# Experts of a mixture-of-experts block: the gated values split on one engine, and four weight splits moved

## The chip, the core and the metric

The kernel runs on one core of one Trainium2 chip. The core has five engines that work side by side, each with its own queue of instructions in program order: TensorE (PE in the rows: matrix products; PEld is its weight load), VectorE (DVE), ScalarE (ACT), GpSimd (POOL) and SyncE (SP, which here only issues transfers). The metric is the device time of one execution in microseconds (us), lower is better, the median of several runs.

## What is computed

One transformer block over 2048 tokens of width 1024, in float32. Token mixers (retention and dilated attention) come first; they take the first three quarters of the time and the change does not touch them. Then every token is routed to 2 of 16 experts, and each expert does

```python
def expert_block(args):
    xblk, e = args
    hid = jax.nn.silu(xblk @ w_gate[e]) * (xblk @ w_up[e])
    return hid @ w_down[e]
```

with `w_gate` and `w_up` 1024 x 512 and `w_down` 512 x 1024 for each expert. The weighted results are added up by token, and a layer norm ends the block.

## The kernel before

**Three products for one.** A float32 product is done as three fast ones. An operand `a` is split into a rounded part `hi` (type fp32r) and a remainder `lo = a - hi`; the product is `hi*hi + hi*lo + lo*hi` (`passes`). `split` (lines 86 to 89) makes the two parts: ACT copies into `hi`, which rounds, and DVE subtracts (lines 88 and 89, which are the lines of every split in the trace, whatever is split).

**One expert after the other.** `MoE.run` goes through 16 experts, each with up to 256 tokens in the main path. For expert e, `blocks` runs four products `gate_up(m)`, m = 0 to 3: 48 matmuls each (line 1286) that give 128 of the 512 gate columns and 128 of the 512 up columns, transposed, side by side in one PSUM bank. After `gate_up(m)` the code writes `hidden(m - 1)` (line 1290): ACT takes silu of the gate half into a tile `s` (L1292), DVE multiplies by the up half (L1293), and `split` puts the parts of the result into `self.h`. Then `part` (line 1313) multiplies by the down weights: first k = 0, 1, 2 for four banks in turn, later k = 3. The very first nine matmuls need `h` of k = 0, 1 and 2 in that order, three matmuls each.

**Two ways to the end of an expert.** If the expert has at most 256 tokens, `two` (line 1550) turns the next expert's gathered tokens (`turn`: 16 transposes at L1261, four banks, each split by ACT and DVE) and then does k = 3. If it has more, `three` (line 1526) does another block of 128 tokens as well. In this run experts 1, 2, 4, 5, 6, 9, 12, 13 and 14 go through `two`, and 3, 7, 8, 10 and 11 through `three`; experts 0 and 15 have code of their own. After either, `rows` scales the four finished banks: ACT does it (L1329) and GpSimd adds the rows to the output in HBM (a scatter that reads and writes, L1229); for e = 3, 7, 11, 15 DVE does it (L1321). The next expert's `gate_up(0)` uses the bank that `rows` reads first.

**Weights.** `weights(n)` (line 1208) splits the next n pieces of the weight queue. A piece is 0.5 MB in one of four raw buffers; ACT and DVE split it, and then SP may ask for the piece that is four further on, into the same buffer (`issue`, L1205 for gate and up, L1206 for down). In the order of the queue, and with names that are used below, an expert's twelve pieces are: D0 to D3, its own down weights (split at m = 0 and m = 1); A0, A1, B0, B1, C0, C1, E0, E1, the next expert's gate and up weights for m = 0, 1, 2, 3. Four further on means: the split of A frees the buffer for C, B for E, C for D0 and D1 of the next expert, E for D2 and D3, D for the next A and B.

**Norms between.** After the experts 3, 7 and 11 a generator `fin` does the last layer norm of finished rows, a step at a time: one after each of m = 0, 1, 2 and one at the end of the expert, through the next three experts. A step is one to three passes of DVE over 1024 columns (L859, L867, L1415, L1417), with small work and a scatter on GpSimd. At m = 2 GpSimd also gathers the next expert's tokens (`fetch`, L1224), after the step's scatter.

In this part every engine works strictly in the order in which the code is written (`manual_schedule`), so an instruction that waits holds up all behind it on its engine.

Of the kernel before, what the change touches and what calls it, by code (L numbers as in the profile page):

```python
# [40 lines left out]
class Ring:  # L41
# [4 lines left out]
    def next(self):  # L46
        v = self.views[self.i % len(self.views)]
        self.i += 1
        return v
# [36 lines left out]
def split(nc, hi, lo, src, sub=None):  # L86

    nc.scalar.activation(hi, src, AF.Copy)  # L88
    (sub or nc.vector).tensor_sub(lo, src, hi)  # L89
# [799 lines left out]
def layer_norm(g, x, st, gain, shift, two):  # L889

    v = g.nc.vector.tensor_add
    for _ in layer_norm_steps(g, x, st, gain, shift, EPS, (g.nc.gpsimd.tensor_add if two else v, v)):
        pass
# [274 lines left out]
class MoE:  # L1168
# [120 lines left out]

    def hidden(self, m, ps):  # L1290
        nc, s = self.g.nc, self.sr.next()
        nc.scalar.activation(s, ps[:, :256], AF.Silu)  # L1292
        nc.vector.tensor_mul(s, s, ps[:, 256:])  # L1293
        split(nc, *(t[:, m, :] for t in self.h), s)

    def down(self, h, idx, tag="main", sums=None, then=None, wait=True):

# [8 lines left out]
    def banks(self, blocks, tag="main"):  # L1306
        return [(b, j, self.g.bank(tag)) for b in blocks for j in range(2)]
# [167 lines left out]
    def blocks(self, e, wg, idx, fin):  # L1475

        p = []
        for m in range(4):
            p.append(self.gate_up(wg[m]))
            if m == 3 and e < NE - 1:  # L1480
                self.hint(e)
            if m:
                self.hidden(m - 1, p[m - 1])
            self.weights((2, 2, 1, 1)[m])
            if m < 3:
                next(fin, None)
            if m == 2:
                self.fetch(e + 1)
                for b in range(2) if e % 4 == 3 else ():
                    self.gather(self.sums[b], self.g.d_z, idx[:, b, 0:1])  # L1490
                if e % 4 == 3 and e < NE - 1:
                    self.list(e // 4)
        return p[3]
# [55 lines left out]

    def two(self, e, ps):  # L1550

        self.weights(4)
        self.turn(e + 1)
        self.part(self.h, ps, (3,))

    def next_block(self, e):
        self.gather(self.xm, self.g.d_x1, self.ir[(e + 1) % 8][:, 2, 0:1])
# [201 lines left out]
```

## Time and profile before

| | |
|---|---|
| median of 3 runs | 3071.51 us (3070.02 to 3075.76) |
| the profiled execution: its time | 3069.23 us |
| its span, first to last instruction | 3067.5 us |
| granted TensorE clock, mean over the span | 0.978 of full |
| the 16 experts | from about 2308 us to the end |

The profile counts busy time by engine, and a busy TensorE hides its waits only if one asks for them. So it is read in three steps: the waits of PE in the experts, the instructions around each of them in order of time, and the transfers that those instructions wait for. Times in rows are microseconds from the start of the span, first the start, then the duration; the bracket is the idle time of the engine just before, and what ended it.

### The profile page before, as it was taken

The page shows a single profiled execution, that of the slowest core. Times are in us where ns is not written, and L with a number is a line of the kernel's source. Part 1 is how long each engine was busy: PE and PEld are TensorE (multiplying, and loading weights), DVE is VectorE, ACT ScalarE, POOL GpSimd, SP SyncE. Part 2 cuts the span into 40 slices and gives each one's busy share as a digit, 9 for nine tenths or more (in the row PEclk, how much of TensorE's full clock was granted, in tenths as well). Part 3 has the DMA queues.
Part 4 walks back from the last instruction along what each step waited for, and adds up shares of the span by engine and source line. Part 5 has one row for each costly group of instructions (what it writes and reads, how often), then busy time and mean ns, then how long its engine had stood idle before and what let it go on. Part 6 is the DMA issues. An engine that isn't in the chain of part 4 may idle for free. (4 is left out here: it accounts for less than half of the span.)

```text
span 3067.5 us, 44091 instructions
## 1 busy us (share of the span) xinstructions
PE 2924.9 (95%) x16140; PEld 2522.2 (82%) x16140; DVE 1427.3 (47%) x3257; ACT 975.4 (32%) x1945; POOL 665.7 (22%) x720
## 2 busy tenths in 40 slices
PE   8999999999999999999889999989998999989996
PEld 6887888888888888888668888878788988878885
DVE  3222433233335523334535666556555476444565
ACT  3221233223333322332123333333224444233342
POOL 0001311122113322100222212222433133122233
PEclk9999999999999999999899999999999999999998
DMA  6445956855776675545854444356737768365684
GB/s 208 147 176 158 201 144 156 182 140 139 157 167 165 174 163 145 143 117 173 287 202 134 155 155 139 127 178 206 145 124 214 253 211 282 112 191 166 208 264 157
DMA packets 449148, 534.16 MB, mean 174 GB/s; under 512 B 183153, under 2 KB 292849, under 8 KB 446818
## 3 DMA queue, kind: packets, MB, share of 16 engines
q1 hardware_dynamic: 261538, 417.78, 42.9%
q0 software_dynamic: 187328, 112.79, 16.1%
q8 instruction: 156, 2.56, 0.4%
q14 instruction: 126, 1.03, 0.1%
HBM read 378.12 MB, written 151.76 MB: 173 GB/s over the span
## 5 line engine op out<-in xcount | busy, mean ns | idle before, releaser
L144 PE MATMUL bank_main<-h,h 128*128 128x512 f32 x3936 | 1022.0, 404 | 9.1 <-ACT h L88 5.3
L144 PEld LDWEIGHTS bank_main<-h,h 128*128 128x128 f32 x3936 | 718.6, 191 | 147.9 <-ACT h L88 7.3
L361 ACT ACTIVATE at<-at,at 128x256 f32<-128x256 f32 (+2 forms) x384 | 174.4, 455 | 542.2 <-DVE at L359 514.6
L1286 PE MATMUL bank_main<-moe,m2w 128*128 128x256 f32 x2304 | 280.2, 283 | 7.5 <-DVE moe L1321 4.8
L1286 PEld LDWEIGHTS bank_main<-moe,m2w 128*128 128x128 f32 x2304 | 278.3, 192 | 10.2 <-issue 6.0
L359 DVE CUSTOM_DVE_ANT_0 at<-bank_att,at 128x256 f32<-128x256 f32 (+2 forms) x384 | 125.0, 363 | 210.7 <-PE bank_att L352 141.4
L1313 PE MATMUL bank_main<-mw,moe 128*128 128x512 f32 x744 | 190.7, 410 | 22.7 <-ACT moe L88 22.6
L1081 PE MATMUL bank_main<-m2w,m 128*128 128x512 f32 x768 | 195.2, 407 | 1.4 <-DVE m L89 1.4
L1313 PEld LDWEIGHTS bank_main<-mw,moe 128*128 128x128 f32 x744 | 141.2, 195 | 60.4 <-ACT moe L88 28.1
L744 PE MATMUL bank_main<-m1r,m1r 128*128 128x512 f32 x672 | 189.7, 415 | 0.0
L379 PEld LDWEIGHTS bank_att<-at,at 128*128 128x128 f32 (+1 forms) x1280 | 168.6, 191 | 15.7 <-DVE at L371 4.3
L1081 PEld LDWEIGHTS bank_main<-m2w,m 128*128 128x128 f32 x768 | 144.1, 193 | 34.3 <-DVE m L89 2.6
L89 DVE TENSOR_TENSOR h<-h,h 128x1024 fp32r<-128x1024 f32 x108 | 133.3, 1239 | 80.6 <-ACT h L88 80.0
L379 PE MATMUL bank_att<-at,at 128*128 128x64 f32 (+1 forms) x1280 | 164.1, 267 | 3.2 <-DVE at L371 3.1
L381 DVE COPY at<-bank_att 128x128 f32<-128x128 f32 x192 | 55.4, 289 | 218.0 <-PE bank_att L379 214.4
L352 PE MATMUL bank_att<-at,at 128*128 128x256 f32 (+2 forms) x768 | 152.9, 326 | 3.8 <-DVE at L381 3.8
L352 PEld LDWEIGHTS bank_att<-at,at 128*128 128x128 f32 x768 | 142.2, 234 | 14.3 <-DVE at L381 4.7
L320 POOL DMA_DIRECT2D at<-d_q x96 | 77.7, 812 | 347.5 <-PE bank_att L352 338.9
L744 PEld LDWEIGHTS bank_main<-m1r,m1r 128*128 128x128 f32 x672 | 125.2, 188 | 25.1
L319 POOL DMA_DIRECT2D at<-d_k x64 | 51.1, 815 | 418.9 <-PE bank_att L352 208.2
L89 DVE TENSOR_TENSOR m2w<-mw,m2w 128x1024 fp32r<-128x1024 f32 x78 | 96.0, 1237 | 94.8 <-ACT m2w L88 89.1
L88 ACT ACTIVATE h<-h 128x1024 fp32r<-128x1024 f32 x108 | 113.4, 1055 | 78.6 <-PE bank_main L144 44.9
(293 smaller groups left out, 4398.4 us busy)
## 6 DMA issues: line engine op xcount, KB each, us to landing
mw<-in_w_gu_dram SPq DMA_DIRECT2D x98, 512.0 KB
h<-in_w_in_dram SPq DMA_DIRECT2D x92, 512.0 KB
mw<-in_w_dn_dram SPq DMA_DIRECT2D x49, 512.0 KB
at<-d_q POOLq DMA_DIRECT2D x96, 256.0 KB
at<-d_k POOLq DMA_DIRECT2D x64, 256.0 KB
at<-d_va SPq DMA_DIRECT2D x240, 64.0 KB
moe<-in_w_gu_dram SPq DMA_DIRECT2D x30, 512.0 KB
d_o<-at SPq DMA_DIRECT2D x192, 66.0 KB
```

Source lines behind the costliest of these rows:

```text
L88: nc.scalar.activation(hi, src, AF.Copy)
L89: (sub or nc.vector).tensor_sub(lo, src, hi)
L144: self.g.nc.tensor.matmul(ps, s[:, k, c], m[:, k % 2, :], start=k + n == 0, stop=k * 3 + n == 23)
L320: done.append(nc.gpsimd.dma_start(Q[i][:, c], ap3(g.d_q, order * 1024 * T + o, [[512 * T, 2], [T, 64], [1, 512]])))
L352: nc.tensor.matmul(ps[:, e, :nk], queries(Q[e]), keys(k), start=n == 0, stop=n == 1)
L359: nc.vector.tensor_tensor_reduce(out=pe, in0=ps[:, e, :nk], in1=bv, scale=1.0, scalar=3e38, op0=OP.add, op1=OP.min, accum_out=ot[:, 128 + ...
L361: nc.scalar.activation(pe, pe, AF.Exp, scale=-1.0, bias=ot[:, 128 + e:129 + e], accum_out=ot[:, 130 + e:131 + e])
L379: nc.tensor.matmul(po[:, 64 * e:64 * e + 64], pt[:cw, e, c, :], v[:cw, c, 64 * e:64 * e + 64], start=c == 0, stop=c == nch - 1)
L744: nc.tensor.matmul(ps, a[:, kk:kk + 128], w[:, c], start=k == ks[0] and i == 0, stop=k == ks[-1] and i == 2)
L1081: nc.tensor.matmul(ps[j], a[:, kk], w[:, c], start=k + i == 0, stop=k * 3 + i == 23)
L1286: nc.tensor.matmul(ps[:, 256 * u:256 * u + 256], x[:, k, c], y[:, k, :], start=k + i == 0, stop=k * 3 + i == 23)
L1313: self.g.nc.tensor.matmul(p, a[:, k, 128 * b:128 * b + 128], w[:, 512 * j:512 * j + 512], start=k + i == 0, stop=k * 3 + i == 11)
```

## The change

`hidden` no longer uses `split`. ACT still does silu. DVE then multiplies twice, once into `hi` (the write rounds) and once in place, and subtracts. ACT's copy of 256 columns is gone, 60 times, and DVE has one more multiplication, 60 times.

Four splits stand elsewhere in each expert, in the same order of pieces: A0 moves from m = 2 to m = 3, in front of A1; in `two`, C0 and C1 move from ahead of `turn` to behind it and behind the last products. (`three` is not changed but for A0.)

```diff
     def hidden(self, m, ps):
         nc, s = self.g.nc, self.sr.next()
+        hi, lo = (t[:, m, :] for t in self.h)
         nc.scalar.activation(s, ps[:, :256], AF.Silu)
+        nc.vector.tensor_mul(hi, s, ps[:, 256:])
         nc.vector.tensor_mul(s, s, ps[:, 256:])
-        split(nc, *(t[:, m, :] for t in self.h), s)
+        nc.vector.tensor_sub(lo, s, hi)
...
-            self.weights((2, 2, 1, 1)[m])
+            self.weights((2, 2, 0, 2)[m])
...
     def two(self, e, ps):
 
-        self.weights(4)
+        self.weights(2)
         self.turn(e + 1)
         self.part(self.h, ps, (3,))
+        self.weights(2)
```

ACT at the end of expert 1, path `two` (B0, B1, C0, C1 are `m2w_14801` and `mw_14981`; the row with x4 is the splitting of the turned tokens; L1329, in the changed kernel L1331, is `rows`; `m2w_14795` is E). Before:

```order
L88 ACTIVATE m2w_14801<-mw_14993 128x1024
L88 ACTIVATE m2w_14801<-moe_17005 128x1024
L88 ACTIVATE mw_14981<-mw_14991 128x1024
L88 ACTIVATE mw_14981<-mw_14992 128x1024
L88 ACTIVATE moe_17022<-bank_att 128x4x128 x4
L1586 UNCONDITIONAL_BRANCH
L1329 ACTIVATE moe_17024<-bank_main,moe_17014 128x512 x4
L88 ACTIVATE m2w_14795<-mw_14993 128x1024
```

and now:

```order
L88 ACTIVATE m2w_14801<-mw_14993 128x1024
L88 ACTIVATE m2w_14801<-moe_17005 128x1024
L88 ACTIVATE moe_17022<-bank_att 128x4x128 x4
L88 ACTIVATE mw_14981<-mw_14991 128x1024
L88 ACTIVATE mw_14981<-mw_14992 128x1024
L1589 UNCONDITIONAL_BRANCH
L1331 ACTIVATE moe_17024<-bank_main,moe_17014 128x512 x4
L88 ACTIVATE m2w_14795<-mw_14993 128x1024
```

The two copies of C now stand between the turned tokens and `rows`.

DVE in expert 4, from the split of D3 (`moe_17005` into `mw_14990`) to the parts of `hidden(2)` (`moe_17010` is `lo` of `h`, `moe_17009` is `hi`; L867, L1415, L859 and L1417 are steps of a norm). Before:

```order
L89 TENSOR_TENSOR mw_14990<-moe_17005,mw_14989 128x1024
L867 BN_AGGR moe_17050<-moe_17050 128x2
L1415 SCALAR_TENSOR_TENSOR moe_17054<-moe_17054,moe_17050,moe_17044 128x1024
L859 BN_STATS moe_17048<-moe_17055 128x6 x2
L1293 TENSOR_TENSOR moe_17026<-moe_17026,bank_main 128x256
L89 TENSOR_TENSOR moe_17010<-moe_17026,moe_17009 128x256
L89 TENSOR_TENSOR m2w_14802<-mw_14991,m2w_14801 128x1024
L1417 SCALAR_TENSOR_TENSOR moe_17054<-moe_17054,moe_17050,moe_17045 128x1024
L867 BN_AGGR moe_17048<-moe_17048 128x2
L1415 SCALAR_TENSOR_TENSOR moe_17055<-moe_17055,moe_17048,moe_17044 128x1024
L1293 TENSOR_TENSOR moe_17025<-moe_17025,bank_main 128x256
L89 TENSOR_TENSOR moe_17010<-moe_17025,moe_17009 128x256
```

and now, from the first multiplication of `hidden(1)` on:

```order
L1294 TENSOR_TENSOR moe_17009<-moe_17026,bank_main 128x256
L1295 TENSOR_TENSOR moe_17026<-moe_17026,bank_main 128x256
L1296 TENSOR_TENSOR moe_17010<-moe_17026,moe_17009 128x256
L1419 SCALAR_TENSOR_TENSOR moe_17054<-moe_17054,moe_17050,moe_17045 128x1024
L867 BN_AGGR moe_17048<-moe_17048 128x2
L1417 SCALAR_TENSOR_TENSOR moe_17055<-moe_17055,moe_17048,moe_17044 128x1024
L1294 TENSOR_TENSOR moe_17009<-moe_17025,bank_main 128x256
L1295 TENSOR_TENSOR moe_17025<-moe_17025,bank_main 128x256
L1296 TENSOR_TENSOR moe_17010<-moe_17025,moe_17009 128x256
L89 TENSOR_TENSOR m2w_14802<-mw_14991,m2w_14801 128x1024
L89 TENSOR_TENSOR m2w_14802<-mw_14992,m2w_14801 128x1024
```

The subtraction for A0 (`m2w_14802` from `mw_14991`) has moved behind `hidden(2)`.

## Rows read from the trace of the kernel before

**Rows 1.** The page: busy time of each engine, its share of the span, and its instructions.

```profile
PE 2924.9 (95%) x16140; PEld 2522.2 (82%) x16140; DVE 1427.3 (47%) x3257; ACT 975.4 (32%) x1945; POOL 665.7 (22%) x720
```

**Rows 2.** Waits of PE from 2334 us, where `gate_up` of expert 1 begins, to the end: the waiting line, the releaser, us in total, times, the longest.

```profile
PE bank_main L1313 <- ACT moe L88: 22.6, 10, 4.7
PE bank_att L1261 <- DMA moe<-d_x,moe: 7.1, 6, 2.1
```

**Rows 3.** Timeline of the end of expert 4 (path `two`), all engines, and the first `gate_up` of expert 5.

```profile
2490.82 1.99 ACT L88 ACTIVATE m2w<-mw 128x1024 fp32r<-128x1024 f32 x2
...
2495.68 1.91 PE L1261 MATMUL bank_att<-const,moe 128*128 128x128 f32 x16
2496.31 2.07 ACT L88 ACTIVATE moe<-bank_att 128x512 fp32r<-128x512 f32 x4 [3.50 <-PE bank_att L1261]
2496.94 2.48 DVE L89 TENSOR_TENSOR moe<-bank_att,moe 128x512 fp32r<-128x512 f32 x4 [2.25 <-ACT moe L88]
2497.34 3.03 PE L1313 MATMUL bank_main<-mw,moe 128*128 128x512 f32 x12
2498.31 2.84 ACT L1329 ACTIVATE moe<-bank_main,moe 128x512 f32<-128x512 f32 x4
2499.98 1.62 POOL L1229 DMA_INDIRECT d_z<-moe,moe  x1 [10.70 <-ACT moe L1329]
2500.20 4.00 PE L1286 MATMUL bank_main<-moe,mw 128*128 128x256 f32 x32
```

**Rows 4.** Timeline at the start of expert 11, after a `three`, where `gate_up` waited for the first bank that `rows` frees.

```profile
2825.17 1.26 ACT L1329 ACTIVATE moe<-bank_main,moe 128x512 f32<-128x512 f32 x2
...
2825.90 6.02 PE L1286 MATMUL bank_main<-moe,m2w 128*128 128x256 f32 x48 [1.35 <-ACT moe L1329]
```

**Rows 5.** Timeline of expert 14: from the copy of D3 to the product that needs `h` of k = 2.

```profile
2981.12 1.06 ACT L88 ACTIVATE mw<-moe 128x1024 fp32r<-128x1024 f32 x1 [2.73 <-DMA moe<-in_w_dn_dram]
...
2982.21 1.23 DVE L89 TENSOR_TENSOR mw<-moe,mw 128x1024 fp32r<-128x1024 f32 x1 [2.56 <-ACT mw L88]
...
2985.99 0.41 DVE L1293 TENSOR_TENSOR moe<-moe,bank_main 128x256 f32<-128x256 f32 x1
...
2987.83 1.23 DVE L89 TENSOR_TENSOR mw<-mw,mw 128x1024 fp32r<-128x1024 f32 x1 [0.52 <-ACT mw L88]
...
2988.97 1.28 DVE L1417 SCALAR_TENSOR_TENSOR moe<-moe,moe,moe 128x1024 f32<-128x1024 f32 x1
...
2991.61 0.41 DVE L1293 TENSOR_TENSOR moe<-moe,bank_main 128x256 f32<-128x256 f32 x1
...
2992.52 7.26 PE L1313 MATMUL bank_main<-mw,moe 128*128 128x512 f32 x30 [2.48 <-ACT moe L88]
```

**Rows 6.** Timeline of PE alone: the same wait in the experts 5, 6, 10 and 13.

```profile
2525.08 7.26 PE L1313 MATMUL bank_main<-mw,moe 128*128 128x512 f32 x30 [0.29 <-ACT moe L88]
...
2564.44 7.26 PE L1313 MATMUL bank_main<-mw,moe 128*128 128x512 f32 x30 [1.40 <-ACT moe L88]
...
2789.12 7.24 PE L1313 MATMUL bank_main<-mw,moe 128*128 128x512 f32 x30 [1.57 <-ACT moe L88]
...
2952.16 7.26 PE L1313 MATMUL bank_main<-mw,moe 128*128 128x512 f32 x30 [1.58 <-ACT moe L88]
```

**Rows 7.** SP's requests for D0 and D1 (one row), D2 and D3 of expert 5, and ACT's copy of D3, which waited for its landing.

```profile
2493.58 1.46 SPq L1206 DMA_DIRECT2D mw<-in_w_dn_dram  x2
...
2503.38 0.33 SPq L1206 DMA_DIRECT2D mw<-in_w_dn_dram  x1
...
2504.52 0.33 SPq L1206 DMA_DIRECT2D moe<-in_w_dn_dram  x1
...
2513.67 1.06 ACT L88 ACTIVATE mw<-moe 128x1024 fp32r<-128x1024 f32 x1 [2.80 <-DMA moe<-in_w_dn_dram]
```

**Rows 8.** Transfers by queue in three windows around it: 2496 to 2499 us (weights alone), 2502 to 2504 us (the first adding scatter alone), 2506 to 2512 us (both). q1 carries SP's transfers, q0 those of GpSimd; packets, MB, and their time as a share of the 16 DMA engines' time in the window.

```profile
q1 hardware_dynamic: 321, 1.18, 99.1%
...
q0 software_dynamic: 66, 0.27, 98.3%
...
q0 software_dynamic: 223, 0.85, 58.5%
q1 hardware_dynamic: 229, 0.87, 42.5%
```

**Rows 9.** Timeline of the experts 9 (two waits) and 11 (ACT's copies of A0 and A1, and PE's wait).

```profile
2743.90 0.97 PE L1313 MATMUL bank_main<-mw,moe 128*128 128x512 f32 x3 [2.09 <-ACT moe L88]
...
2749.53 8.75 PE L1313 MATMUL bank_main<-mw,moe 128*128 128x512 f32 x30 [4.65 <-ACT moe L88]
...
2851.78 1.06 ACT L88 ACTIVATE m2w<-mw 128x1024 fp32r<-128x1024 f32 x1 [3.17 <-DMA mw<-in_w_gu_dram]
...
2854.78 1.04 ACT L88 ACTIVATE m2w<-mw 128x1024 fp32r<-128x1024 f32 x1
...
2854.93 8.81 PE L1313 MATMUL bank_main<-mw,moe 128*128 128x512 f32 x30 [4.34 <-ACT moe L88]
```

**Rows 10.** Timeline of expert 15: the gather of the last norms' rows, and the first pass of DVE over them.

```profile
3026.86 0.97 POOL L1224 DMA_INDIRECT moe<-d_z,moe  x1 [11.21 <-DMA moe<-d_gslot]
...
3031.20 1.29 DVE L859 BATCH_NORM_STATS2 moe<-moe 128x6 f32<-128x512 f32 x2 [5.90 <-DMA moe<-d_z,moe]
...
3037.17 12.67 PE L1313 MATMUL bank_main<-mw,moe 128*128 128x512 f32 x42 [2.90 <-ACT moe L88]
```

## Prediction

> **What bounds the kernel now.** PE is busy 95% of the span [rows 1], so only its waits can be won, and new waits lost. The change touches experts 1 to 15. There PE's largest wait is for `h`: 22.6 us in ten waits at the first products with the down weights [rows 2]; next is the wait of `turn` for gathered tokens, 7.1 us. These two lists are read first. Then the timeline around one such wait shows why it is there [rows 5]. D3 lands late, ACT copies it at 2981.12 (call this t), and all that follows stands behind it in order: DVE's subtraction for D3, a step of a norm, `hidden(1)` at t + 4.87, the split of A0, another step of a norm, `hidden(2)` at t + 10.49, ACT's copy, and PE at t + 11.40. Both ACT and DVE are idle by turns there, and still it is one chain, tied to the landing of one transfer. The experts 5, 6, 10 and 13 wait at the same place [rows 6], 9 and 11 at it or just before [rows 9].
>
> **The change, part by part: `hidden` and A0.** On DVE `hidden` was two operations of 0.41 to 0.42 with a wait for ACT between; it becomes three. Their prices are the rows of the same shapes, 0.41 us from a PSUM operand [rows 5]. The second and third have no other engine to wait for. From t, `hidden(1)` starts at t + 4.87 as before and takes 3 x 0.41 to t + 6.10. The subtraction for A0 (1.14, from 2987.83 to 2988.97) is out of the way. The step of the norm takes 2.64 (2988.97 to 2991.61), to t + 8.74, and the first multiplication writes `hi` 0.41 later. PE can go on at t + 9.15 instead of t + 11.40: 2.25 saved. The remainder now comes two operations after `hi`, 0.82, where PE wants it after two matmuls of 0.24 (7.26 / 30) [rows 5]; 0.35 of that shows, so 1.9 net, and I take 2.0, with 1.7 to 2.3 as bounds. The new wait of the subtraction on its own engine is taken at nothing: the nearest row is the step in which DVE goes from one pass to the next [rows 5] without a gap. ACT loses 60 copies that it could not start early anyway.
>
> [...]
>
> **C behind `turn`.** ACT's copies of C0 and C1 now stand between the turned tokens and `rows`. At the end of expert 4 [rows 3] the four copies of turned tokens run from 2496.31 to 2498.38, the first `rows` begins at 2498.31, and PE starts the next expert at 2500.20, at once behind its last product: `rows` had about 1.2 us to spare (2498.31 + 0.69 = 2499.00). Two copies at a pace of 0.95 (two take 1.99 [rows 3]) push the first `rows` to 2500.2, done at 2500.9, and PE starts 0.04 after that, as it did where `rows` did bind: 2825.17 + 0.69 against 2825.90 [rows 4]. So PE waits about 0.75 us where it waited for nothing. That is at each of nine experts; in one (6) the turn itself ran late enough to hide it by my reading. 8 x 0.75 = **+6.0**, bounds 0 and 9 x 0.8.
>
> **Where C's buffers go.** D0 and D1 of the next expert are asked for when C's splits are done. Before: at 2493.58 and 1.1 later, ahead of `turn`, and they crossed while GpSimd's queue was empty [rows 7, 8]: alone, weights move at 321 packets in 3 us, or 128 (0.5 MB) in 1.2. Now DVE subtracts for C0 after the turned tokens (2496.94 + 2.48 = 2499.42), so D0 is asked for at about 2500.7 and D1 at 2501.9, just as the adding scatter begins. That scatter is slow: 66 packets in 2 us fill the engines to 98% [rows 8], so its 128 take 3.9 us. Where both queues have work they go packet for packet, 223 against 229, whatever each packet costs [rows 8]. Before, the first scatter ran alone, D2 beside the gather that follows it, D3 beside the second scatter, and D3 was copied at 2513.67 [rows 7]. Now D1 runs beside the first scatter, D2 and D3 as before. The first scatter starts 1.8 later (its `rows` does) and takes 1.2 longer (D1's packets between), so D3 lands 3.0 later, 2.3 later counted from the start of its expert. Bounds: 0.9 (if D0 and D1 get through before the scatter's packets come) and 3.5.
>
> In the five experts that had the chain of [rows 5] behind a `two` (5, 6, 10, 13, 14) the 2.0 saved meets the 2.3 lost: 5 x 0.3 = **+1.5** (bounds -5 and +8). In four of them (10 takes the other path) `turn` also waits for gathers that GpSimd issues after the same step of the norm: 1.8 earlier against 2.3 later, and C's transfers now run beside them, since A0 and A1 are split later: 4 x 0.5 = **+2.0** (0 to 4), an estimate.
>
> **Where D3 does not move.** Experts 9 and 11 follow a `three`, which keeps its order. Expert 9 waits 2.09 and 4.65 [rows 9]; its second wait falls by about 2.2 less the 0.35: **-1.8**. In expert 11 ACT stood 3.17 for A0 ahead of the silu of `hidden(2)` [rows 9]; now it does not, and the 4.34 goes, with the slower matmuls after it (30 in 8.81 against 7.26). But A1 is now copied ahead of the silu of `hidden(3)`, at about 2854.8, and the fourth bank of the down products is the one that `hidden(3)` must have read. PE comes to it at 2855.3 (6.3 after the products' start at 2849.0) and it is free at about 2858: 2.7 of wait next in line. **-3.0**, bounds -5.9 and -1.5.
>
> Expert 15's norms hang on transfers behind the same scatters: the gather at 3026.86 waited 11.21, DVE another 5.90, and PE then 2.90 [rows 10]. They move with the scatters, 2.3 later, less about 0.4 for the shorter `hidden`: **+1.9** (bounds -0.9 and +3).
>
> **Sum.** 6.0 + 1.5 + 2.0 - 1.8 - 3.0 + 1.9 = +6.6 us. On the profiled execution's own time, 3069.2, that gives 3075.8. That execution lies 2.3 below the median of the runs shown, 3071.5; on the median it is **3078.1**, or 3078 (+0.2%). A difference under 0.2%, 6.1 us, is about what a measurement of this kernel cannot tell from none; the forecast stands just at this line.
>
> **Rivals.**
> 1. *D3 lands no later* (the ring of four buffers absorbs the late request). For it: in the rows D0 and D1 were there long before their copies. Against it: the queues are full from 2502 to 2512 [rows 8]. Then the five experts win what they waited, at most 2.0 each: 0.3 + 1.4 + 1.6 + 1.6 + 2.0 = 6.9, about 2 more in slow matmuls behind such waits, and expert 15 wins 0.9: 6.0 - 6.9 - 2 - 1.8 - 3.0 - 0.9 = -8.6, **3063**, faster.
> 2. *D0 and D1 get through ahead of the scatter*, D3 moves by only 0.9. The five win about 1.1 each (0.3 in expert 5): 6.0 - 4.7 - 1.8 - 3.0 + 0.5 = -3.0, **3068.5**, no change to be told.
> 3. *C lands late for its new place.* ACT in order then holds `rows` for C1, and PE for `rows`. C1 is asked for after `hidden(2)` and two subtractions, at about t + 12.3 or 28.0 after the expert's start; ACT wants it at about 37. D3, asked for at 2504.52, took 9.1 us to its copy beside scatters [rows 7]; a C1 beside two gathers that takes as long is just in time, and from there each us is PE's. At 2 us in each of the four experts 5, 6, 13, 14 it is +8: **3086**, slower.
> That the change does not do what it says is ruled out by the order of the instructions.
>
> **How the numbers follow.** Forecast, 3074 to 3082: 0.50, of which I count 0.28 above the line of +6.1 and 0.22 below. Rival 1: 0.13 (0.11 faster, 0.02 same). Rival 2: 0.17 (0.15 same, 0.02 faster). Rival 3: 0.20, slower. Together: faster 0.13, same 0.39, slower 0.48. The range leaves out rival 1 and the end of rival 3: 3067 to 3088.
>
> **What would show it.** In the profile of the changed kernel: L1286 waiting 0.6 to 0.8 us for ACT's `rows` at the starts of the experts 2, 3, 5, 6, 10, 13, 14, 15 (the first term); ACT's copy of D3 some 16 us after its expert's start instead of 13.5 (the second); PE behind that copy by 9.2 instead of 11.4 (`hidden`); no 4.34 in expert 11, but a wait inside its down products for a bank that DVE reads. No wait for `rows`, or D3 at its old place, would make the forecast wrong by 6 or by 10.

## The result, and the profile after

The changed kernel takes **3094.0 us** (median of 6 runs, 3086.9 to 3100.2) against 3071.7 us (6 runs, 3066.5 to 3075.8) for the kernel before on the same chip: a ratio of **1.0071**, 95% interval 1.0059 to 1.0084. It is slower, as forecast, by 22 us and not by 7, and lies above the range. The profiled execution took 3093.0 us, with a span of 3091.1.

The page's busy line answers to [rows 1]: PE works 10 us more for the same instructions, and the span is 24 us longer.

```profile
PE 2935.3 (95%) x16140; PEld 2529.4 (82%) x16140; DVE 1451.9 (47%) x3317; ACT 952.1 (31%) x1885; POOL 675.6 (22%) x720
```

The waits of PE from 2334 us to the end, as in [rows 2] (waiting line, releaser, us in total, times, the longest). L1315 is the old L1313 (products with the down weights), L1294 writes `hi`, L1295 the second product, L1331 is `rows`, L1508 the branch to `three` or `two`.

```profile
PE bank_att L1261 <- DMA moe<-d_x,moe: 22.6, 10, 3.7
PE bank_att L1261 <- PEq L1508: 10.9, 4, 3.9
PE bank_main L1315 <- DVE moe L1294: 6.6, 4, 2.5
PE bank_main L1286 <- ACT moe L1331: 4.9, 6, 1.4
...
PE bank_main L1315 <- DVE moe L1295: 1.9, 1, 1.9
```

The wait for `h`, 22.6 us before, is down to 6.6 and 1.9: the change does what it is for, and more than I gave it. The wait of `turn` for gathered tokens is up from 7.1 to 22.6.

PE's groups from 2343 us to the end, first of before, then of after (count, busy us, mean ns of one, idle time and its releasers):

```profile
L1313 PE MATMUL bank_main<-mw,moe 128*128 128x512 f32 x720 | 184.9, 410 | 22.7 <-ACT moe L88 22.6
L1261 PE MATMUL bank_att<-const,moe 128*128 128x128 f32 x272 | 37.7, 288 | 15.3 <-DMA moe<-d_x,moe 7.1 <-PEq L1506 6.5 <-DVEq L1510 1.1
```

```profile
L1315 PE MATMUL bank_main<-mw,moe 128*128 128x512 f32 x720 | 193.3, 425 | 8.8 <-DVE moe L1294 6.6 <-DVE moe L1295 1.9 <-DVE moe L1296 0.4
L1261 PE MATMUL bank_att<-const,moe 128*128 128x128 f32 x272 | 39.9, 298 | 35.1 <-DMA moe<-d_x,moe 22.6 <-PEq L1508 10.9 <-DVEq L1512 1.1
```

The same matmuls take 8.4 + 2.2 us longer. They are the ones that stand right behind a wait: behind the turn of expert 13 (below) twelve products of L1315 have a median of 628 ns, where it was 396. With these rows the books close. From PE's start on expert 1 (2334.0 before, 2338.7 after) to the end of the span it is 733.5 us before and 752.4 after, **18.9** more. Gathers +15.5, slower matmuls +10.6, branch +4.4 (6.5 before), `rows` +2.2 (2.7 before), `h` 8.9 - 22.6 = -13.7: together 19.0. The other 4.7 us of the span lie ahead of expert 1, in expert 0, which the change hardly touches: PE stands 3.68 us ahead of the last transpose there with no releaser shown, where it stood 0.82, and the 24 products behind it take 8.50 us where they took 5.85. The profiles of the kernels in the experiments 1, 2 and 4 below, with the change's parts and without, begin expert 1 between 2334.7 and 2342.8 (the kernel before with earlier gathers stands 3.49 us at the same transpose), so I take it for a difference between executions, and not for the change's.

**Where the gathers wait.** Expert 13 before: GpSimd's two gathers of the next tokens (L1224), SP's requests for the four weight pieces C0, C1, E0 (one row) and E1, and `turn` (L1261).

```profile
2948.72 9.17 SPq L1205 DMA_DIRECT2D mw<-in_w_gu_dram  x3
...
2953.50 1.73 POOL L1224 DMA_INDIRECT moe<-d_x,moe  x1 [0.19 <-issue]
2955.54 0.96 POOL L1224 DMA_INDIRECT moe<-d_x,moe  x1 [0.31 <-issue]
2958.70 0.33 SPq L1205 DMA_DIRECT2D moe<-in_w_gu_dram  x1
2960.27 1.06 PE L1261 MATMUL bank_att<-const,moe 128*128 128x128 f32 x8 [0.85 <-DMA moe<-d_x,moe]
...
2961.73 1.09 PE L1261 MATMUL bank_att<-const,moe 128*128 128x128 f32 x8 [0.39 <-DMA moe<-d_x,moe]
```

The same in the changed kernel, with the products behind it:

```profile
2970.81 3.85 SPq L1205 DMA_DIRECT2D mw<-in_w_gu_dram  x3
2971.40 1.43 POOL L1224 DMA_INDIRECT moe<-d_x,moe  x1 [0.19 <-issue]
2973.14 2.00 POOL L1224 DMA_INDIRECT moe<-d_x,moe  x1 [0.31 <-issue]
2975.46 0.33 SPq L1205 DMA_DIRECT2D moe<-in_w_gu_dram  x1
2980.63 1.30 PE L1261 MATMUL bank_att<-const,moe 128*128 128x128 f32 x8 [3.68 <-DMA moe<-d_x,moe]
...
2983.07 1.97 PE L1261 MATMUL bank_att<-const,moe 128*128 128x128 f32 x8 [1.14 <-DMA moe<-d_x,moe]
...
2984.69 4.59 PE L1315 MATMUL bank_main<-mw,moe 128*128 128x512 f32 x12
```

The expert begins at 2926.0 before and at 2945.3 after. Counted from there the second gather is asked for at 29.6 before and at 27.9 after, 1.7 earlier; its tokens are turned at 35.7 before and at 37.8 after, 2.1 later. It took 6.2 us, and takes 9.9. Before, the four weight pieces are asked for over 10 us; now, with A0 and A1 split together and B right behind them, within 5 us, about the two gathers. The queues in the 8 us from the first gather's request on (before 2953.5 to 2961.5 us, after 2971.4 to 2979.4; packets, MB, share of the 16 engines; q0 is GpSimd's):

```profile
q0 software_dynamic: 357, 1.27, 42.8%
q1 hardware_dynamic: 214, 0.80, 32.1%
```

```profile
q1 hardware_dynamic: 391, 1.46, 60.9%
q0 software_dynamic: 182, 0.65, 23.2%
```

GpSimd's queue moved 182 packets where it had moved 357, weights 391 where they had moved 214. The even counts of [rows 8], 223 and 229, are not met here.

And the clock: the 12 last products at 2984.69 take 4.59 us; they took 3.05 before. The windows from the first of these turns to the next expert, before and after (length, busy us and counts of PE, PEld, DVE, ACT and POOL, then the granted clock, DMA share, GB/s):

```profile
2960.30:2965.50 5.20, 4.81 (x29) 4.02 (x30) 3.48 (x5) 4.04 (x7) 0.27 (x1) 1.00 0.98 377
```

```profile
2980.60:2989.30 8.70, 7.53 (x30) 6.26 (x31) 5.11 (x6) 6.01 (x9) 0.30 (x1) 0.61 0.24 84
```

The granted clock was 1.00 there and is 0.61 after PE had stood for 3.68 us; from 2981.32 to 2988.15 us it is 0.50. The wait came with more than its own 3.68 us: the 12 products behind it took 1.54 longer.

### The profile page after: what moved, and what is told of

Its sections match the earlier page's. It is cut to its first block, busy times and chain, and to the rows that moved or that the text cites. A ratio compares the mean times of both kernels' runs of the same rounds, so it can differ in the third digit from the quotient of the medians.

```text
span 3091.1 us, 44170 instructions
## 1 busy us (share of the span) xinstructions
PE 2935.3 (95%) x16140; PEld 2529.4 (82%) x16140; DVE 1451.9 (47%) x3317; ACT 952.1 (31%) x1885; POOL 675.6 (22%) x720
## 3 DMA queue, kind: packets, MB, share of 16 engines
q0 software_dynamic: 187328, 112.79, 15.7%
## 5 line engine op out<-in xcount | busy, mean ns | idle before, releaser
L1315 PE MATMUL bank_main<-mw,moe 128*128 128x512 f32 x744 | 201.8, 429 | 8.8 <-DVE moe L1294 6.6
L1315 PEld LDWEIGHTS bank_main<-mw,moe 128*128 128x128 f32 x744 | 150.6, 208 | 50.7 <-DVE moe L1294 8.1
L379 PEld LDWEIGHTS bank_att<-at,at 128*128 128x128 f32 (+1 forms) x1280 | 168.8, 192 | 14.8 <-DVE at L371 3.4
L352 PEld LDWEIGHTS bank_att<-at,at 128*128 128x128 f32 x768 | 142.1, 234 | 13.9 <-DVE at L381 4.2
## 6 DMA issues: line engine op xcount, KB each, us to landing
at<-d_q POOLq DMA_DIRECT2D x96, 256.0 KB, 12.2
```

The source lines that it names most:

```text
L352: nc.tensor.matmul(ps[:, e, :nk], queries(Q[e]), keys(k), start=n == 0, stop=n == 1)
L379: nc.tensor.matmul(po[:, 64 * e:64 * e + 64], pt[:cw, e, c, :], v[:cw, c, 64 * e:64 * e + 64], start=c == 0, stop=c == nch - 1)
L1315: self.g.nc.tensor.matmul(p, a[:, k, 128 * b:128 * b + 128], w[:, 512 * j:512 * j + 512], start=k + i == 0, stop=k * 3 + i == 11)
```

## The experiments

All ratios are to the kernel before, on the same chip, with 95% intervals; the chip is another from experiment to experiment (two in the fourth), so kernels of different experiments are compared through the kernel before. The sums of waits come from one profiled execution of each kernel.

**1. Which part of the change.** Four kernels: the new `hidden` alone (`hid`), the moves of A0 and of C alone (`moves`), and the new `hidden` with each move:

```diff
 hidden: new in hid, hid_a, hid_c; old in moves
-            self.weights((2, 2, 1, 1)[m])      # A0 moved: hid_a, moves
+            self.weights((2, 2, 0, 2)[m])
...
-        self.weights(4)                         # C moved: hid_c, moves
+        self.weights(2)
         self.turn(e + 1)
         self.part(self.h, ps, (3,))
+        self.weights(2)
```

> Only the new hidden: both parts of the gated values formed on VectorE, all weight splits where they were. Theory G (gathers): what the change lost is the wait of the turn for gathered tokens, 7.1 us before and 22.6 after, and it comes from A0's later split, which asks for C0 beside the gathers. Then this kernel has C0 early and the shorter chain: the waits for h fall from 22.6 to under 9 us, the gather waits stay under 12, no wait for rows, and the time is 5 to 10 us under the kernel before. Theory R (the recorded one: rows and D): it wins as well, 8 to 12 us, so this run tells little between them but sizes the gain of the new hidden.

> Only the four moved splits, with the old hidden (ScalarE still rounds). Theory G: C0 is asked for even later than in the full change, since hidden(2) comes later, so the gather waits are 20 us or more, and waits for h stay above 10: 20 to 30 us slower than before. Theory R: 6 us of waits for rows and a later D3 add to the waits for h, about 12 to 16 us slower, with gather waits of about 9.

> The new hidden and A0 moved from m = 2 to m = 3, but C0 and C1 still split ahead of the turn. Theory G: C0 is asked for as late as in the full change; gather waits of 15 to 25 us, no waits for rows: 12 to 20 us slower than before. Theory R: no cost of C left, so as fast as the new hidden alone or faster, 5 to 10 us under the kernel before.

> The new hidden, and C0 and C1 behind the turn, but A0 still at m = 2. Theory G: C0 is asked for early and has landed before the gathers start: gather waits under 12 us, waits for rows of 0.5 to 0.6 at eight experts: within 4 us of the kernel before. Theory R: nearly all the cost is here, 15 to 22 us slower than before.

| kernel | ratio | `turn` for gathers | `h` | `rows` | branch, and nothing shown |
|---|---|---|---|---|---|
| before | 1 | 7.1 | 22.6 | 2.7 | 6.5 |
| hid | 1.0017 (1.0008 to 1.0027) | 15.7 | 17.0 | 2.7 | 5.8 + 2.7 |
| moves | 1.0021 (1.0006 to 1.0036) | 16.7 | 12.2 | 5.1 | 7.5 + 4.4* |
| hid_a | 1.0036 (1.0023 to 1.0049) | 22.2 | 9.0 | 2.7 | 11.6 |
| hid_c | 1.0048 (1.0033 to 1.0062) | 17.5 | 15.6 | 4.9 | 5.7 + 3.4 |
| changed | 1.0071 (1.0059 to 1.0084) | 22.6 | 8.9 | 4.9 | 10.9 |

\* At the branch of expert 11; the profile puts it down to another gather (`moe<-d_z`). PE goes on 3.1 us behind the start of a packet of the instruction queue there, as it does at other branches (experiment 4), so I count it with these; which of the two it waited for is not shown.

Both theories had the new `hidden` win by itself, and it does not: it loses 0.17%. Each step that shortens the wait for `h` lengthens the wait for gathers, with A0's move or without. So the meeting of A0 with the gathers, which I had named as the cause, is not all of it. In expert 5 of `hid` the second gather is asked for at 30.3 after the expert's start and turned at 40.5: 10.2 us, with all splits in their old places. The weights have come closer to the gathers there too. E1 and the next D0 are asked for 2.9 and 4.1 us behind the first gather, where it was 5.2 and 6.3, and in the 8 us from that gather's request on the queues moved, first before (2526.42 to 2534.42), then in `hid` (2533.43 to 2541.43):

```profile
q0 software_dynamic: 366, 1.30, 42.9%
q1 hardware_dynamic: 226, 0.85, 34.4%
```

```profile
q1 hardware_dynamic: 298, 1.11, 50.3%
q0 software_dynamic: 257, 0.94, 35.8%
```

So the shorter `hidden` by itself brings the weights' transfers onto the gathers, and A0's move adds to it.

**2. The gathers earlier.** GpSimd works in order, and the two gathers stand behind the norm's step of m = 2: in expert 13 a scatter that waits for DVE (2.50 us before, 0.75 after) and two small operations. They are asked for at m = 1 instead, in the changed kernel, in the kernel before, and in `hid` and `hid_a`. The step of m = 1, which waits longer for DVE (9.81 us before, 7.87 after), stays ahead of them. In expert 13 the first gather goes out 19.1 us after the expert's start instead of 27.5 in the kernel before, and 22.5 instead of 26.1 in the changed one.

```diff
+            if m == 1:
+                self.fetch(e + 1)
             if m == 2:
-                self.fetch(e + 1)
                 for b in range(2) if e % 4 == 3 else ():
```

> The changed kernel, with the two gathers of the next expert's tokens asked for one step earlier in the expert (behind the step m = 1 and not m = 2, some 8 us earlier). Theory G (the time went into `turn` waiting for gathers that cross beside C and E): those waits, 22.6 us in the changed kernel, fall below 6, the h waits (6.6) grow by at most 4, and the ratio to the kernel before falls from 1.007 to about 1.002 (1.000 to 1.004). Rival T (the transfers of an expert together set the pace, whichever is late is waited for): the gather waits fall, but D3 and with it the h waits grow by nearly as much, 10 us or more; the ratio stays at 1.005 to 1.008.

> Only the new `hidden`, all splits in their old places, and the two gathers one step earlier. Theory G: gather waits from 15.7 to below 5, h waits at most 18 (15.8 without the earlier gathers); ratio 0.996 to 0.999, against 1.0017 with the gathers in their old place. Rival T: the h waits grow to about 25, ratio 1.001 to 1.003.

> The new `hidden` and A0 moved behind it, C in its old place, the two gathers one step earlier. Theory G: gather waits from 22.2 to below 6, h waits at 6 to 10; ratio 0.995 to 0.998, the fastest of the four if the time lay in the gathers. Rival T: h waits 15 or more, ratio 1.002 to 1.005.

> The kernel before with the two gathers one step earlier and nothing else. Theory G: gather waits from 7.1 to about 2, h waits unchanged at 20 to 25; ratio 0.997 to 0.999. Rival T: h waits up by 5 to 10, ratio 1.000 to 1.002.

Waits of the changed kernel with the earlier gathers, and of the kernel before with them (the view of [rows 2]):

```profile
PE bank_att L1261 <- PEq L1509: 9.4, 4, 4.6
PE bank_main L1315 <- DVE moe L1294: 8.1, 4, 2.2
PE bank_att L1261 <- issue: 7.1, 3, 2.9
PE bank_main L1286 <- ACT moe L1331: 6.5, 9, 1.4
```

```profile
PE bank_main L1313 <- ACT moe L88: 18.6, 8, 4.7
PE bank_att L1261 <- PEq L1507: 5.1, 4, 3.0
```

No wait for these gathers is left in either, and `h` is not late for it: 22.6 to 18.6 before, 8.9 to 10.1 in the changed kernel. Ratios: changed **0.9985** (0.9967 to 1.0003), that is 0.86% or 26 us better than the change alone; kernel before **0.9944** (0.9926 to 0.9962); `hid` 0.9931 (0.9908 to 0.9954); `hid_a` 0.9947 (0.9928 to 0.9966). The rival, that the transfers together set the pace, falls: the gathers come earlier and nothing else comes later by as much. The 7.1 us of [rows 2], with what hung on it, was worth 17 us, which I had not seen in it. Of the change's 0.71% the gathers' old place carries 0.86 - 0.56 = 0.30%, with an interval of about 0.28% either way; 0.41% between the two kernels is left.

**3. Less weight traffic.** To tell crowding from late asking, most of E0 and E1 is not loaded:

```diff
             if kind == "gu":
-                return self.g.nc.sync.dma_start(r.rearrange("p (k c) -> p k c", k=4), self.g.w_gu[e, m, :, 4 * j:4 * j + 4, :])
+                n = 8 if e > 1 and m == 3 else 128
+                return self.g.nc.sync.dma_start(r[:n].rearrange("p (k c) -> p k c", k=4), self.g.w_gu[e, m, :n, 4 * j:4 * j + 4, :])
```

> The changed kernel, leaving out most of the two loads of the last quarter of each expert's gate and up weights from expert 2 on (8 of 128 partitions are loaded, the rest of the buffer holds old weights); requests, copies, splits and matmuls stay. Theory G (gathers and PE's own code cross beside the weights asked for at the same time): the waits of `turn` for gathers fall from 22.6 us to below 8, and PE's waits at the branch and for nothing shown (10.9 + 3.7) to below 8; ratio to the kernel before about 0.997. Rival L (the gathers are late because they are asked for late, behind the norm): gather waits stay at 18 or more, ratio above 1.003.

> The kernel before with the same loads left out, as the measure of what less traffic gives by itself. Theory G: gather waits from 7.1 to below 3, ratio 0.993 to 0.997, so that the changed kernel stands 0.2 to 0.4% above this one, and not 0.7%. Rival L: the changed kernel stands 0.6% or more above this one.

1.0029 (1.0012 to 1.0045) and 1.0008 (0.9992 to 1.0024): they stand 0.21% apart (0.23% either way) and not 0.71%, as the crowding would have it, but the gather waits fall only to 15.9 and not below 8, and the kernel before gains nothing (9.4 us of gather waits for 7.1). So both hold in part. Without E's traffic the second gather lands 8.7, 8.4 and 7.5 us after its request in the experts 5, 6 and 14, where it took 9.6, 9.4 and 9.2; in 13 all tokens are turned in one go from 35.1 us after the start. And PE still stands 2 to 4 us for them, since it comes to `turn` soon after they were asked for: in expert 13 at 32.1, the second gather being asked for at 28.8.

**4. What is left: 0.4%.** First the rival that it lies with D. The third gather of an expert stood between the two adding scatters of [rows 8]; it is put behind the two others, with a small GpSimd operation in its old place (`self.gap` is its tile):

```diff
             if m == 1:
                 self.fetch(e + 1)
+                if e > 1:
+                    self.next_block(e - 1)
...
-                self.rows(ps, idx[:, :2], self.sums if last else None, then=lambda: self.next_block(e))
+                self.rows(ps, idx[:, :2], self.sums if last else None, then=lambda: nc.gpsimd.tensor_scalar_add(self.gap, g.neghalf, 0.0))
```

> The kernel before with the two gathers one step earlier, and the third gather of each expert (the tokens of a possible third block, 512 KB, so far between the two adding scatters at the expert's start) put behind them, where the queues are freer; a small GpSimd operation stands in its old place. Theory Q (D3 lands late because GpSimd's transfers cross beside it packet for packet; 128 fewer of them): the copy of D3 in expert 5 comes at 12 to 13.3 us after the expert's start, against 14.6 with the gather in its old place; h waits fall from 18.6 to 6 to 12; ratio 0.990 to 0.993. Rival W (D3 waits for the adding scatters, whose packets are slow, and not for the gather): D3 within 0.5 of 14.6, h waits 16 or more, ratio 0.994 to 0.997.

> The same with the new `hidden` (all splits in their old places). Theory Q: D3 copied at 13 to 14.5 after the start of expert 5, against 15.8; h waits from 13.9 to 3 to 8; ratio 0.988 to 0.992. Rival W: D3 within 0.5 of 15.8, h waits 12 or more, ratio 0.992 to 0.995.

> The new `hidden`, C0 and C1 behind `turn`, A0 in its old place, the two gathers one step earlier. Theory S (C's place costs by itself: `rows` behind its copies, and PE's code fetched beside weights that are asked for later): waits for `rows` 5 to 7 us (2.7 without), ratio 0.995 to 0.998, that is 0.2 to 0.5% above the same kernel with C in its old place (0.993). Rival I (C costs only together with A0's move, which leaves the two to ask for their buffers at the same time): ratio 0.991 to 0.9945.

> The old `hidden`, the moves of A0 and of C, the two gathers one step earlier. Theory S (the moves cost the same with either `hidden`): ratio 0.998 to 1.001, 0.4 to 0.6% above the kernel before with the earlier gathers alone (0.994). Rival H (the shorter `hidden` is what lets PE run into late transfers, and without it the moves cost little): 0.994 to 0.9965.

> The changed kernel with the two gathers one step earlier and the third gather behind them. Theory S: what the moves cost stays with all gathers out of the way; ratio 0.997 to 1.000 (0.994 without the moves). Rival Q (what is left of the cost in the changed kernel with earlier gathers lies in D0 and D1, which are asked for later and cross beside the gather that is moved here): D3 of expert 5 copied before 13.5 after the start, ratio 0.992 to 0.9955.

| with earlier gathers | ratio | `h` | `rows` | branch, and nothing shown |
|---|---|---|---|---|
| kernel before | 0.9944 (0.9926 to 0.9962) | 18.6 | 2.7 | 5.1 |
| hid | 0.9931 (0.9908 to 0.9954) | 15.0 | 2.7 | 3.6 + 6.1 |
| moves | 0.9942 (0.9923 to 0.9960) | 11.0 | 7.7 | 6.4 + 4.6* |
| hid_c | 0.9976 (0.9962 to 0.9991) | 17.5 | 7.5 | 7.5 + 4.8 |
| changed | 0.9985 (0.9967 to 1.0003) | 10.1 | 6.5 | 9.4 + 7.1 |
| kernel before, third gather too | 0.9928 (0.9915 to 0.9941) | 14.0 | 5.9 | 6.1 |
| hid, third gather too | 0.9943 (0.9924 to 0.9962) | 14.6 | 3.5 | 6.5 + 4.3 |
| changed, third gather too | 0.9986 (0.9970 to 1.0002) | 10.5 | 6.9 | 11.1 + 11.6 |

\* As in experiment 1: at the branch of expert 11, put down to another gather.

D3 of expert 5 is copied at 12.4 after the expert's start (14.5 without the third gather's move) in the kernel before, at 12.6 (15.8) in `hid`, which is what theory Q said of D3. But `h` waited 14.0 and 14.6 where I said 6 to 12 and 3 to 8, since most of what is left, some 12 us in either, stands in the experts 9, 11 and 15. The changed kernel does not gain by it, and its `h` does not fall (10.1 to 10.5), so its rest is not at D. With the old `hidden` the moves cost nothing (0.9942 against 0.9944): `rows` +5.0, `h` -7.6, and +5.9 at the branch with the wait of expert 11, in a profiled execution (3065.7) that is one of its two longest (median 3060.0). With the new one C's move costs 0.45%, more than `rows` explains. Theory S is half right, rival H is right, and neither says why.

What the kernels with the new `hidden` and earlier gathers have, and those with the old one do not, is a wait of PE at the first transposes of `turn` with no releaser shown, in two or three of the experts 5, 9 and 13 (`hid` and `hid_c` of experiment 1 have one each). Expert 13 of `hid` with earlier gathers, and the instruction queue's one packet in the quarter of a microsecond from 2957.00:

```profile
2959.73 1.94 PE L1261 MATMUL bank_att<-const,moe 128*128 128x128 f32 x16 [2.08 <-issue]
```

```profile
q8 instruction: 1, 0.02, 22.0%
```

PE goes on 2.5 to 2.7 us behind the start of that packet of 16 KB, and so it does in all twenty such waits of the nine kernels that have them (2.51 to 2.66 by the packets' starts). The waits at the branch look alike: in the experts 10 and 11 PE goes on 3.0 and 3.15 us behind the start of such a packet in the changed kernel, where it stands 3.94 and 3.34, and 3.1 behind it at both in the kernel before (2.98 and 0.94).

**5. PE's code shifted.** If it is PE's own code that arrives late, the wait hangs on where the code is cut. 64 or 32 transposes of the identity in expert 0 (each a weight load and a matmul) shift it by 128 or 64 instructions; nothing later changes.

```diff
-    def to_t(self, x, xt, c):
+    def to_t(self, x, xt, c, more=0):          # 64 or 32 in expert 0, else 0
...
+            for i in range(0 if j else more):
+                g.nc.tensor.transpose(ps[:, :128], g.ident, g.ident)
```

> The new `hidden` with the earlier gathers, and 64 transposes of the identity (each a weight load and a matmul; their result is overwritten) put on PE in expert 0, where it stands 12 us for gathered tokens, so that all later code of PE lies 128 instructions further on. Theory K (what PE waits for at the first transposes of `turn` in the experts 5, 9 and 13 with no releaser shown is its own code: a piece of 16 KB that ends just there): these waits, 6.1 us in three places, are gone there or stand elsewhere; below 2 us at `turn`, ratio 0.991 to 0.9935. Rival N (they belong to the shorter chain of `hidden`, not to where the code is cut): still 5 to 7 us at the same three places.

> The changed kernel with the earlier gathers and the same 64 transposes. Theory K: the waits with no releaser shown, 7.1 us at `turn` in the experts 5, 9, 13, fall below 2; the ratio falls from 0.9985 to 0.995 to 0.9975. Rival N: they stay at 6 to 8 at the same places, ratio 0.998 to 0.9995.

> The same with 32 transposes, 64 instructions. Theory K: the piece of code ends at another place than in the two others, so the waits with no releaser differ from both in size or place. Rival N: as without the transposes.

Expert 13 of `hid` with 64 transposes (its gathers are asked for at 21.4 and 23.7 after the start, 21.7 and 24.0 without), and expert 6 of the changed kernel with 64:

```profile
2964.42 1.91 PE L1263 MATMUL bank_att<-const,moe 128*128 128x128 f32 x16
```

```profile
2583.51 1.94 PE L1263 MATMUL bank_att<-const,moe 128*128 128x128 f32 x16 [1.40 <-issue]
```

The waits are gone from 5, 9 and 13 in all three. In the changed kernel with 64 transposes they stand in 6 and 14 instead (1.40 and 1.51), with 32 nowhere. Theory K holds for the waits. What they cost is less clear. Ratios: `hid` 0.9964 (0.9947 to 0.9980), changed 0.9988 (0.9975 to 1.0001) with 64 and 0.9961 (0.9946 to 0.9976) with 32. The transposes cost time themselves, which I had not meant: they landed behind expert 0's gate and up products and not in its wait for tokens, and 64 of them take 9.8 us there in `hid` and 8.6 in the changed kernel, 32 take 6.3. So the profiles are compared from PE's start on expert 1 to the end: `hid` 719.2 to 718.1; changed 728.9 to 726.8 with 64, to **717.3** with 32; the kernel before with earlier gathers has 717.5. In one layout, then, the changed kernel is as fast from there as the kernel before, in the two others it is not. These are single executions, and those of the changed kernel with earlier gathers lie between 3060.3 and 3087.1 us; but the ratios put the three layouts in the same order. With the transposes' time taken off, as if all of it showed (an estimate), they are 0.9960 with 64 and 0.9941 with 32, against 0.9985 without and 0.9944 for the kernel before. For `hid` it is 0.9932 against 0.9931: there 6.1 us of waits went, and nothing was won.

## Why the prediction was wrong, step by step

**The step that failed is the sum's term for the gathers, "4 x 0.5 = +2.0 (0 to 4), an estimate".** I knew that `turn` waits for gathers that follow the same step of the norm, and that C's transfers would run beside them, and I priced both at half a microsecond. Measured: 15.5 us more waiting, in five experts and not four (9 has 3.7, after a `three`), and most of 10.6 us of slower matmuls behind waits. Two things were left out. A gather's way from request to `turn` (6.8 and 6.2 us in the rows of before, 9.2 and 9.9 in those of after) gets no shorter when PE waits less for `h`, so what PE gains there is given back at `turn`. And A0's later split puts four weight requests into the gathers' 5 us, after the shorter `hidden` alone has brought the weights closer. Experiment 2 shows the first; the queues' packets show the second, and experiment 3 bears it out in part. By the ratios the gathers' old place carries 0.30% of the 0.71%, and not all that the waits add up to: with the gathers on time PE meets what comes next, `rows`, the branch and its own code.

**`hidden` was right to the hundredth in expert 14.** The rows after, answering to [rows 5], t = 3003.76:

```profile
3003.76 1.06 ACT L88 ACTIVATE mw<-moe 128x1024 fp32r<-128x1024 f32 x1 [2.47 <-DMA moe<-in_w_dn_dram]
...
3008.63 0.40 DVE L1294 TENSOR_TENSOR moe<-moe,bank_main 128x256 fp32r<-128x256 f32 x1
3009.06 0.42 DVE L1295 TENSOR_TENSOR moe<-moe,bank_main 128x256 f32<-128x256 f32 x1
3009.52 0.43 DVE L1296 TENSOR_TENSOR moe<-moe,moe 128x256 fp32r<-128x256 f32 x1
...
3012.15 8.56 PE L1315 MATMUL bank_main<-mw,moe 128*128 128x512 f32 x36
3012.50 0.41 DVE L1294 TENSOR_TENSOR moe<-moe,bank_main 128x256 fp32r<-128x256 f32 x1
```

`hidden(1)` starts at t + 4.87 and `hidden(2)` at t + 8.74, both as worked out; PE has its 36 products in one row, without a wait. The two passes that read the bank take 0.40 and 0.42, the one that does not 0.43, so the price from [rows 5], 0.41, was the right one.

**D3 "2.3 later" was wrong.** Expert 5 after, answering to [rows 3, 7]:

```profile
2507.89 2.44 ACT L1331 ACTIVATE moe<-bank_main,moe 128x512 f32<-128x512 f32 x4
2508.36 4.53 SPq L1206 DMA_DIRECT2D mw<-in_w_dn_dram  x3
2508.64 6.02 PE L1286 MATMUL bank_main<-moe,mw 128*128 128x256 f32 x48 [0.56 <-ACT moe L1331]
...
2522.53 1.06 ACT L88 ACTIVATE mw<-moe 128x1024 fp32r<-128x1024 f32 x1 [3.21 <-DMA moe<-in_w_dn_dram]
```

D0 is asked for 0.3 before the expert's start, as forecast, but D3 is copied 13.9 after it, against 13.5 before. In the experts 5, 6, 10, 13 and 14 it is 13.9, 14.7, 14.5, 14.3 and 14.6; before, 13.5, 14.6, 14.7, 14.8 and 15.7. ACT waited instead for D0 and D1, 0.6 to 3.7 us, and PE waited for neither. So the condition of rival 1 held, and the five experts won all 7.3 us of their wait for `h`. Its time of 3063 did not come, because it, too, took the gathers for on time.

**`rows` had the right mechanism and too large a price.** PE waits 0.51 to 0.58 us, not 0.75, and in the experts 2, 3, 5 and 13 only: in 6, 10, 14 and 15 `turn` ran late enough to hide it, which I had seen for one. Together +2.2 and not +6.0. With the gathers on time it shows at more of them: 6.5 to 7.7 us against 2.7.

**Expert 11** answers to [rows 9]: the 4.34 is gone, the wait at the bank is there as forecast (1.87 for 2.7), and then PE stands 3.34 at the branch, where it stood 0.94.

```profile
2874.76 3.55 PE L1315 MATMUL bank_main<-mw,moe 128*128 128x512 f32 x9 [1.87 <-DVE moe L1295]
...
2881.66 1.31 PE L1261 MATMUL bank_att<-const,moe 128*128 128x128 f32 x8 [3.34 <-PEq L1508]
```

Expert 9 gained 2.9 at `h` (6.74 to 3.71 and 0.18; I said 1.8) and lost 3.7 at its gathers. Expert 15 did not get longer by 1.9: from its start to the end it is 59.3 us before and 58.1 after, since D3 came no later (14.6 after the start, 14.8 before). Against the forecast, then: `rows` 3.8 better, `h` some 9, expert 15 about 3; the branch 4.4 worse, which had no term, the gathers and the matmuls behind the waits 24 worse. The small errors on the good side hid nothing: one term was short by more than all the others together.

**What stays open.** Of the 0.41% that is left with the gathers on time, the shifted code shows that PE's waits with no releaser are its own code, and in one layout of three the whole rest is gone with them. Why the layout with 64 transposes keeps 9 us more in its profile than that with 32 (0.19% by the ratios), whose waits differ by only some 5, is not settled; nor is PE's wait at the branch (6.5 to 10.9 us): the packets ahead of it point to code there too, but no run here tests it, and in the shifted layouts it stays (9.7 and 10.9).

## What to carry to other kernels

A wait that is taken away is won only up to the next thing that PE must have: before pricing it, follow the path to the next join (here `turn`), take the landing of what is needed there as a time of its own, and count from it. Requests that PE will wait for should leave ahead of work that they do not need: GpSimd's gathers, asked for one step earlier than a norm's, are worth 0.56% on the kernel before, 0.72% with the third gather too; that version (0.9928) has none of the change in it, and none here is faster by more than the intervals. And a wait costs more than itself where the matmuls behind it run at a granted clock of 0.61, as the twelve products that took 4.59 us for 3.05.

## What the hardware showed unexpectedly

PE can wait for its own code in the middle of straight work: 1.4 to 4.3 us at one transpose, 2.5 to 2.7 us behind the start of a 16 KB packet of the instruction queue, and moving the code by 64 or 128 instructions moves the wait to other experts or takes it away. An edit on DVE and ACT alone brought these waits to PE in the experts 5, 9 and 13 (6.1 us in `hid` with earlier gathers, none in the kernel before with them), so two kernels that differ by a few instructions can differ by several microseconds that have nothing to do with the edit's purpose.
